# Recurrent gates of an encoder block: a full-height block-diagonal matmul against two 64-row halves

## The chip, the cores and the metric

The kernel runs on one core of one Trainium2 chip. The metric is the device time of one execution in microseconds (us), as the median of several executions. PE is the matrix engine (TensorE), PEld its weight loads, DVE the vector engine, ACT the scalar engine, POOL GpSimd, SP the engine that issues most DMAs. PSUM is the memory that PE writes its results to, eight banks of 128 partitions by 512 float32.

## What is computed

One layer of a streaming encoder on 512 frames of 1024 features: an RMS norm, one wide projection, a banded attention branch, a recurrent branch, a gated merge, and a SwiGLU feed-forward. The part that the change touches is the gates of the recurrent branch. The recurrent input (after a causal convolution of width 4) has 1024 features in 16 blocks of 64, and each gate multiplies each block by a 64 by 64 matrix of its own:

```
def rg_lru(x, w_r, b_r, w_i, b_i, lam):
    B, S, D = x.shape
    xb = x.reshape(B, S, N_RG_BLOCKS, RG_BLOCK)
    r = jax.nn.sigmoid(jnp.einsum('bsnd,nde->bsne', xb, w_r).reshape(B, S, D) + b_r)
    i = jax.nn.sigmoid(jnp.einsum('bsnd,nde->bsne', xb, w_i).reshape(B, S, D) + b_i)
    log_a = -RG_C * r.astype(jnp.float32) * jax.nn.softplus(-lam.astype(jnp.float32))
    a = jnp.exp(log_a)
    mult = jnp.sqrt(-jnp.expm1(2.0 * log_a))
    bx = mult * (i * x).astype(jnp.float32)
...
    _, h = lax.associative_scan(combine, (a, bx), axis=1)
    return h.astype(x.dtype)
```

## The kernel before

Features lie on partitions, frames along the free dimension. The 1024 features are eight feature tiles of 128 partitions, j = 0 to 7, so a feature tile holds two blocks of 64. Every product is made in three matmuls, because each float32 operand is kept as a rounded high part and a low remainder: high by high, high by low, low by high (`mm3`, L72 to L76). A projection of one feature tile is eight such triples, 24 matmuls of 128 rows by 512 columns into one PSUM bank.

**The recurrent stage.** The loop at L572 goes over j = 0, 2, 4, 6. For each it projects the recurrent input of two feature tiles (`xr`), convolves them (`rnn_conv`, L481: one ACT, three DVE instructions), and splits the result into a high part on ACT (L491) and a low part on POOL (L492), the tile `xch`. Then it projects the two GeLU gates (`gr`), and after each of them makes the recurrent gates of that feature tile (`rnn_gates`, L504). Then come the merge gates (`ga`, `gb`).

**The recurrent gates.** At setup the two gate weights are laid out as block-diagonal 128 by 128 matrices, one for each feature tile: a tile `wrg_raw` for each gate is set to zero on POOL (L322), two DMAs from SP fill the diagonal blocks (L324, L325), ACT rounds the whole tile to its high part (L470), and POOL subtracts to get the low part (L471). In `rnn_gates` each of the two gates takes one triple (L508) into a PSUM bank of its own (tag "s", two banks) and is read by one ACT instruction, a tanh with a bias from `hb` over 128 partitions by 512 (L510). After that ACT (L516, L517), DVE (L519 to L530) and POOL (L521, L535) make the recurrence out of it.

**PSUM.** One pool `ps` has four banks with the tag "mm", two with "t" (transposes and the `gr` projections), two with "s". The two "s" banks hold at first `gm_p` (the transposed norm gain, L379), then the gates, later the attention scores (L653), one of the feed-forward products (L275) and pieces of the output (L954).

**Order.** The instructions of an engine run in the order in which a planner has put them, from priorities and a model of the time; each then waits only for its own inputs and buffers. In the attention stage the order on PE is fixed by hand (L734). ACT, DVE and POOL work through their queues in order.

Also in `norm_half` (L343): the scaled input `xs` (DVE, L349) is transposed on PE (L357) into tiles with the tag "t", and split to `xnT` by ACT (L361) and DVE (L362).

Of the kernel before, what the change touches and what calls it, by code (L numbers as in the profile page):

```python
# [20 lines left out]
HD = 64  # L21
# [15 lines left out]
def block_kernel(ctx: ExitStack, tc: tile.TileContext, x, norm_mix_g, w_in, b_merge, rel_table,  # L37
# [3 lines left out]
    pe, dve, act, pool, sp = nc.tensor, nc.vector, nc.scalar, nc.gpsimd, nc.sync  # L41
# [9 lines left out]
    top = ctx.enter_context(pool_of("top", 1, "right"))  # L51
    top.tile([P, 120], F32, name="top_fill")
    cp = ctx.enter_context(pool_of("cp"))
    cp.tile([P, 48], F32, name="cp_fill")
    wp = ctx.enter_context(pool_of("wp", 2))
    tg_ = ctx.enter_context(pool_of("tg", 2))
    xn_stack, xnp = opened("xnT")
    nm_stack, nm = opened("norm")
# [1 line left out]
    qk_stack, qkp = opened("qk", 3, "right")  # L60
    z_stack, zp = opened("z", 1, "right")
    rw2_stack, rw2 = opened("rw2", 2, "right")
    ps = ctx.enter_context(tc.tile_pool(name="ps", bufs=2, space=PSUM))
    dr = ctx.enter_context(tc.tile_pool(name="dr", bufs=1, space=bass.MemoryType.DRAM))

    def f(ap):
        return ap.bitcast(F32)

    def mm_tile(name, tag="mm"):
        return ps.tile([P, S], F32, tag=tag, bufs=4 if tag == "mm" else 2, name=name)  # L70

    def mm3(o, sh, sl, mh, ml, start, stop, parts=False):  # L72

        pe.matmul(o, sh, mh, start=start, stop=False, skip_group_check=parts)  # L74
        pe.matmul(o, sh, ml, start=False, stop=False, skip_group_check=parts)  # L75
        pe.matmul(o, sl, mh, start=False, stop=stop, skip_group_check=parts)  # L76
# [194 lines left out]
    def block_product(name, i, right, c):  # L271

        w = weights(name)
        p = ps.tile([P, 256], F32, tag="mm", bufs=4, name=f"p_{name}")
        q = ps.tile([P, 2, 256], F32, tag="st"[i % 2], bufs=2, name=f"q_{name}")  # L275
# [40 lines left out]
    for t in range(2, NT):  # L316
        sp.dma_start(out=xt[t][:], in_=x[t * P:(t + 1) * P, :])
    load("gr0", 0)
    wrg_raw = []
    for name, w in (("r", w_rg_r), ("i", w_rg_i)):  # L320
        raw = nm.tile([P, 8, P], F32, name=f"wrg_raw_{name}")
        pool.memset(raw[:], 0.0)  # L322
        pairs = w.rearrange("(t two) d e -> two d t e", two=2)
        sp.dma_start(out=raw[0:64, :, 0:64], in_=pairs[0])  # L324
        sp.dma_start(out=raw[64:128, :, 64:128], in_=pairs[1])  # L325
        wrg_raw.append(raw)
    vr = nm.tile([NV, P], F32, name="vr")
    sp.dma_start(out=vr[V_CW:V_CW + 32, :], in_=conv_w.rearrange("w (t p) -> (w t) p", p=P))
    for at, vec, n in ((V_CB, conv_b, 8), (V_BR, b_rg_r, 8), (V_BI, b_rg_i, 8), (V_LAM, rg_lambda, 8), (V_BM, b_merge, 16),
# [46 lines left out]
        act.activation(junk[:], xt[t][:], AF.Square, accum_out=q[:])  # L376
        ssq.append(q[:])

    gm_p = ps.tile([P, S], F32, tag="s", bufs=2, name="gm_p")  # L379
    pe.transpose(gm_p[:, 0:8], gm_r[:], ident[0:8, 0:8])  # L380
    gm = cp.tile([P, 8], F32, name="gm")
    act.copy(gm[:], gm_p[:, 0:8])
    _, xnT = features(xnp, "xn", "xnT")
# [25 lines left out]
    pe.transpose(vp[:, 0:NV], vr[:], ident[0:NV, 0:NV])  # L409
    vc = cp.tile([P, NV], F32, name="vc")  # L410
    dve.tensor_copy(vc[:], vp[:, 0:NV])
    hb = cp.tile([P, 32], F32, name="hb")
    dve.tensor_scalar(hb[:, 0:16], vc[:, V_BR:V_BR + 16], 0.5, None, ALU.mult)
    dve.tensor_scalar(hb[:, 16:32], vc[:, V_BM:V_BM + 16], 0.5, None, ALU.mult)
    gf = vc[:, V_GF:V_GF + 8]


# [46 lines left out]
    sp2, spm4 = softplus_neg()  # L464


    wrg = []
    for name, raw in zip("ri", wrg_raw):
        hl = rw2.tile([P, 2, 8, P], F32R, bufs=1, name=f"wrg_{name}")
        act.activation(hl[:, 0], raw[:], AF.Copy)  # L470
        pool.tensor_sub(hl[:, 1], raw[:], f(hl[:, 0]))  # L471
        wrg.append(hl)

    nm_stack.close()

    rw_stack, rw = opened("rw", 2)


    u_pairs = []
# [22 lines left out]
        return g  # L502

    def rnn_gates(j, xc, xch, g):  # L504
        gates = []
        for n in range(2):
            po = ps.tile([P, S], F32, tag="s", bufs=2, name=f"rg{j}_{n}")
            mm3(po[:], wrg[n][:, 0, j], wrg[n][:, 1, j], xch[:, 0], xch[:, 1], True, True)  # L508
            gt = rw.tile([P, S], F32, tag=f"gt{n}", bufs=(2, 3)[n], name=f"gt{j}_{n}")
            act.activation(gt[:], po[:], AF.Tanh, bias=hb[:, 8 * n + j:8 * n + j + 1], scale=0.5)  # L510
            gates.append(gt)
        tr, ti = gates
        if j % 2 == 0:
            u_pairs.append(rw.tile([P, 2, S], F32, tag="u", bufs=2, name=f"u{j}"))
        u = u_pairs[-1][:, j % 2]
        act.activation(u, tr[:], AF.Tanh, bias=sp2[:, j:j + 1], scale=sp2[:, j:j + 1])  # L516
        act.activation(tr[:], tr[:], AF.Exp, bias=spm4[:, j:j + 1], scale=spm4[:, j:j + 1])  # L517

        dve.scalar_tensor_tensor(u, tr[:], 1.0, u, ALU.add, ALU.mult)  # L519
        a = rw.tile([P, S], F32, tag="a", bufs=3, name=f"a{j}")  # L520
        pool.tensor_scalar(a[:], u, -1.0, 1.0, ALU.mult, ALU.add)  # L521

# [49 lines left out]
    for j in range(0, KT, 2):  # L572
        for c in range(2):
            conv[j + c] = rnn_conv(j + c, tile_of(f"xr{j}", c, ahead=2))
        for c in range(2):
            po = tile_of(f"gr{j}", c, "mm" if j == 0 else "t")
# [13 lines left out]
    def halves(e):  # L590
        own, other = slice(e * HD, e * HD + HD), slice(HD - e * HD, 2 * HD - e * HD)
        return own, other


    qk = {}

# [48 lines left out]
    def scores(h):  # L645
        pr, e = divmod(h, 2)
        q, kh, kl = qk[pr]
        bias = bias_tile(h)
        lsum = cp.tile([P, NT], F32, tag="lsum", bufs=2, name=f"l{h}")
        nmax = cp.tile([P, NT], F32, tag="nmax", bufs=2, name=f"m{h}")  # L650
        rl = cp.tile([P, NT], F32, tag="rl", bufs=2, name=f"rl{h}")
        prob = [aw2.tile([P, (qb + 1) * P], F32, tag=f"p{qb}", name=f"p{h}_{qb}") for qb in range(NT)]
        banks = [ps.tile([P, S], F32, tag="s", bufs=2, name=f"s{h}_{i}") for i in range(2)] + [mm_tile(f"s{h}_2")]  # L653
        scs = [banks[0][:, 0:P], banks[0][:, P:3 * P], banks[1][:, 0:3 * P], banks[2][:]]
        for qb in range(NT):
            w = (qb + 1) * P
            qs = q[:, e, qb * P:(qb + 1) * P]
            pe.matmul(scs[qb], qs, kh[:, e, 0:w], start=True, stop=False)
            pe.matmul(scs[qb], qs, kl[:, e, 0:w], start=False, stop=True)
        for qb in range(NT):  # L660
            w = (qb + 1) * P
            dve.tensor_tensor_reduce(prob[qb][:], scs[qb], bias[:, S - w:S], -1.0, 3e38, ALU.add, ALU.min, nmax[:, qb:qb + 1])  # L662
            act.activation(prob[qb][:], prob[qb][:], AF.Exp, bias=nmax[:, qb:qb + 1], scale=-1.0, accum_out=lsum[:, qb:qb + 1])  # L663
        dve.reciprocal(rl[:], lsum[:])  # L664
        for qb in range(NT):
            pool.tensor_scalar(prob[qb][:], prob[qb][:], rl[:, qb:qb + 1], 1.0, ALU.mult, ALU.mult)  # L666
        return prob
# [283 lines left out]
    for cc, tags in enumerate(("mmmm", "sstmm")):  # L951

        pieces = [(t, every) for t in range(NT)] if cc == 0 else [*((t, every) for t in range(3)), (3, slice(0, CW)), (3, slice(CW, S))]
        pos = [ps.tile([P, S], F32, tag={"m": "mm"}.get(tag, tag), bufs=4 if tag == "m" else 2, name=f"po_out{cc}_{i}")  # L954
               for i, tag in enumerate(tags)]
        for k0 in ks[:late] if cc else ks:
            if cc == 0:
                for i in range(max(1, k0 // 2), min(k0 + 4, FT) // 2):
                    split_act(i)
            wf = weights(f"fo{cc}_{k0}", 3)  # L960
            for (t, at), po in zip(pieces, pos):
                out_tile(t, po, k0, wf, at)
        if cc == 0:
            for (t, at), po in zip(pieces, pos):
                h_out(0, t, po, pool, 0, at)
    wfs = [weights(f"fo1_{k0}", 0) for k0 in ks[late:]]
    for i, ((t, at), po) in enumerate(zip(pieces, pos)):
        for k0, wf in zip(ks[late:], wfs):
            out_tile(t, po, k0, wf, at)
        n = 1 + i // 4  # L970
# [30 lines left out]
```

## Time and profile before

| | us |
|---|---|
| median of 3 executions (881.80 to 882.15) | 881.89 |
| the profiled execution | 881.99 |
| its span, from the first instruction to the last | 880.2 |
| PE busy in the span | 869.7 |
| PE weight loads | 776.3 |
| DVE busy | 546.7 |
| ACT busy | 472.4 |
| POOL busy | 111.2 |
| DMA, mean over the span | 102 GB/s |

Busy time of PE is the union of its matmuls' records. A record is longer than the distance to the next one, since the matmuls are pipelined, so the distance between starts is the cost of one, and the length of the record is that plus a tail. The recurrent stage lies between about 34 and 180 us. The attention stage follows to about 440 us, the merge and the feed-forward take the rest.

### The profile page before, as it was taken

The numbers are of one execution on the slowest core, as the hardware profiler recorded it, in microseconds if no ns is written. First come the engines' busy times: TensorE is split into PE (matmuls) and PEld (weight loads), VectorE is DVE, ScalarE is ACT, GpSimd is POOL, SyncE is SP. The second block draws the span as 40 slices with busy tenths as digits, with TensorE's granted clock in tenths as the row PEclk, the third lists the DMA queues.
The fourth block names the chain that finished last, engine by engine and source line by source line (L and its number), as shares of the span: only waits on it lengthen the run. The fifth ranks groups of instructions, "written<-read, shape, count | busy, mean of one in ns | idle before, by whom it ended". The sixth has DMA issues, their size and how long they took to land.

```text
span 880.2 us, 13310 instructions
## 1 busy us (share of the span) xinstructions
PE 869.7 (99%) x5220; PEld 776.3 (88%) x5220; DVE 546.7 (62%) x856; ACT 472.4 (54%) x823; POOL 111.2 (13%) x141
## 2 busy tenths in 40 slices
PE   8999999999999999999999999999999999999997
PEld 5988888888888999988888889999999999888886
DVE  5776557663366676665556557888888887554203
ACT  7666656662256776666533366555555555723103
POOL 4013211220011222322100000000000001301100
PEclk9999999999999999999999999999999999999999
DMA  8223232433342232321223630433333332353002
GB/s 268 82 87 98 93 96 81 136 96 95 101 139 74 89 90 83 86 73 60 73 96 114 245 95 27 144 95 121 98 96 99 117 121 73 127 182 121 25 1 96
DMA packets 86079, 90.10 MB, mean 102 GB/s; under 512 B 5376, under 2 KB 74608, under 8 KB 86016
## 3 DMA queue, kind: packets, MB, share of 16 engines
q1 hardware_dynamic: 84640, 85.78, 31.4%
q10 hardware_dynamic: 1376, 3.47, 1.0%
q8 instruction: 41, 0.67, 0.3%
q14 instruction: 22, 0.18, 0.1%
HBM read 87.10 MB, written 2.14 MB: 101 GB/s over the span
## 4 chain that ended last, share of the span: by engine, by line
PE 97%; DVE 1%; ACT 1%; issue 1%; DMA 0%; ACTq 0%
PE po_out L74 5%; PE po_out L76 5%; PE po_out L75 5%; PE p_fg L74 2%; PE o L697 2%; PE p_fg L76 2%; PE p_fu L76 2%; PE p_fu L75 2%; PE p_fg L75 2%; PE p_fu L74 2%; PE pT L677 2%; PE po_v L74 2%; PE po_v L76 2%; PE po_v L75 2%; PE po_ga L74 2%; PE po_q L74 2%
## 5 line engine op out<-in xcount | busy, mean ns | idle before, releaser
L75 PE MATMUL po_out<-whl_fo,act_hi 128*128 128x512 f32 (+1 forms) x198 | 72.5, 366 | 0.0
L74 PE MATMUL po_out<-whl_fo,act_hi 128*128 128x512 f32 (+1 forms) x198 | 72.3, 366 | 0.0
L76 PE MATMUL po_out<-whl_fo,act_lo 128*128 128x512 f32 (+1 forms) x198 | 71.7, 365 | 0.0
L666 POOL TENSOR_SCALAR p<-p,rl 128x128 f32<-128x128 f32 (+1 forms) x64 | 39.7, 638 | 128.8 <-DVE rl L664 128.5
L81 DVE TENSOR_TENSOR whl_fo<-raw_fo,whl_fo 128x1024 fp32r<-128x1024 f32 x22 | 27.8, 1274 | 44.2 <-ACT whl_fo L80 43.8
L885 POOL TENSOR_TENSOR act_lo<-act,act_hi 128x1024 fp32r<-128x1024 f32 x4 | 10.9, 2716 | 323.5 <-ACT act_hi L884 321.5
L80 ACT ACTIVATE whl_fo<-raw_fo 128x1024 fp32r<-128x1024 f32 x22 | 23.0, 1058 | 49.0 <-PE po_out L76 34.6
L663 ACT ACTIVATE p<-p,m 128x128 f32<-128x128 f32 (+1 forms) x64 | 35.8, 560 | 16.1 <-DVE m L662 16.1
L76 PEld LDWEIGHTS po_out<-whl_fo,act_lo 128*128 128x128 f32 x198 | 37.3, 189 | 6.0
L75 PEld LDWEIGHTS po_out<-whl_fo,act_hi 128*128 128x128 f32 x198 | 37.4, 189 | 5.9
L74 PEld LDWEIGHTS po_out<-whl_fo,act_hi 128*128 128x128 f32 x198 | 37.4, 189 | 5.9
L74 PE MATMUL po_v<-whl_v,xnT 128*128 128x256 f32 x128 | 36.8, 287 | 0.0
L76 PE MATMUL po_v<-whl_v,xnT 128*128 128x256 f32 x128 | 36.2, 283 | 0.0
L75 PE MATMUL po_v<-whl_v,xnT 128*128 128x256 f32 x128 | 36.2, 283 | 0.0
L81 DVE TENSOR_TENSOR pp<-pT,pp 128x384 fp32r<-128x384 f32 (+1 forms) x48 | 27.9, 598 | 8.5 <-ACT pp L80 8.5
L662 DVE CUSTOM_DVE_ANT_0 p<-s,bias 128x128 f32<-128x128 f32 (+1 forms) x64 | 29.1, 484 | 0.0
L75 PE MATMUL po_xr<-xnT,whl_xr 128*128 128x512 f32 (+1 forms) x80 | 27.9, 354 | 0.6 <-DVE xnT L362 0.6
L81 DVE TENSOR_TENSOR whl_fg_s<-s_fg,whl_fg_s 128x1024 fp32r<-128x1024 f32 x20 | 25.6, 1294 | 3.7 <-ACT whl_fg_s L80 3.7
L74 PE MATMUL po_gr<-xnT,whl_gr 128*128 128x512 f32 (+1 forms) x80 | 27.8, 349 | 0.1
L76 PE MATMUL po_gr<-xnT,whl_gr 128*128 128x512 f32 (+1 forms) x80 | 27.5, 348 | 0.3 <-DVE whl_gr L81 0.3
L75 PE MATMUL po_gr<-xnT,whl_gr 128*128 128x512 f32 (+1 forms) x80 | 27.6, 347 | 0.0
L81 DVE TENSOR_TENSOR whl_qk<-raw_qk,whl_qk 128x1024 fp32r<-128x1024 f32 x16 | 20.8, 1298 | 10.8 <-ACT whl_qk L80 10.8
(352 smaller groups left out, 3041.1 us busy)
## 6 DMA issues: line engine op xcount, KB each, us to landing
raw_fg<-in_w_ffn_in_dram SPq DMA_DIRECT2D x24, 512.0 KB, 4.1
raw_fu<-in_w_ffn_in_dram SPq DMA_DIRECT2D x22, 512.0 KB, 3.7
raw_fo<-in_w_ffn_out_dram SPq DMA_DIRECT2D x22, 512.0 KB, 4.1
raw_qk<-in_w_in_dram SPq DMA_DIRECT2D x32, 256.0 KB, 3.7
raw_xr<-in_w_in_dram SPq DMA_DIRECT2D x8, 512.0 KB, 4.6
raw_gr<-in_w_in_dram SPq DMA_DIRECT2D x8, 512.0 KB, 3.4
raw_ga<-in_w_in_dram SPq DMA_DIRECT2D x8, 512.0 KB, 3.9
raw_gb<-in_w_in_dram SPq DMA_DIRECT2D x8, 512.0 KB, 3.4
```

The lines of the kernel that those rows point to most:

```text
L74: pe.matmul(o, sh, mh, start=start, stop=False, skip_group_check=parts)
L75: pe.matmul(o, sh, ml, start=False, stop=False, skip_group_check=parts)
L76: pe.matmul(o, sl, mh, start=False, stop=stop, skip_group_check=parts)
L80: act.activation(hi, src, AF.Copy)
L81: dve.tensor_sub(lo, src, f(hi))
L662: dve.tensor_tensor_reduce(prob[qb][:], scs[qb], bias[:, S - w:S], -1.0, 3e38, ALU.add, ALU.min, nmax[:, qb:qb + 1])
L663: act.activation(prob[qb][:], prob[qb][:], AF.Exp, bias=nmax[:, qb:qb + 1], scale=-1.0, accum_out=lsum[:, qb:qb + 1])
L666: pool.tensor_scalar(prob[qb][:], prob[qb][:], rl[:, qb:qb + 1], 1.0, ALU.mult, ALU.mult)
L677: pe.transpose(pt[:, at * P:(at + 1) * P], prob[qb][:, kb * P:(kb + 1) * P], ident[:])
L697: pe.matmul(po[:, S - n:S], st, pp[i][:, part, lo:lo + n], start=kb == 0 and part == 0, stop=kb == NT - 1 and part == 1)
L885: (pool if i in (0, 1, 2, 4) else dve).tensor_sub(lo[:], o[:], f(hi[:]))
```

## The change

The two blocks of a feature tile are no longer one block-diagonal matrix of 128 rows. Block e (0 or 1) lies on rows 64e to 64e+63. Its weights for both gates stand side by side on these rows, 64 columns for each gate, so that one matmul of 64 rows and 128 columns gives both gates of one block. For block 0 the gate r has the columns 0 to 63, for block 1 the columns 64 to 127, so r of a block always comes out on the partitions where the block's features lie, and i on the other 64.

For each feature tile there are six matmuls again: the three products of the splitting, each for the two blocks, alternating between the rows 64 to 127 and the rows 0 to 63. The results go to a tile of two PSUM banks, one bank for each block, out of a pool of its own (`rg`, one buffer). The order of the six on PE is fixed, and the products with the low part of `xch` come first. The two gates are read by four ACT instructions of 64 partitions where there were two of 128; those for i read from one half of the partitions and write to the other, with a copy of the bias that is swapped in the same way (eight more columns of `hb`, two more small DVE copies).

One weight tile of 128 by 8 by 128 takes the place of two. The two POOL memsets go, the four DMAs stay, and one ACT rounding and one POOL subtraction remain of two each. The PSUM banks of the gates are given back after the recurrent stage to a pool `ss`, which the attention scores and the later users of "s" use. `gm_p` moves to a "t" bank. Two small constant tiles (`cp_fill`, `hb`) change their widths so that the memory behind them keeps its place.

```diff
-    cp.tile([P, 48], F32, name="cp_fill")
+    cp.tile([P, 40], F32, name="cp_fill")
...
-    ps = ctx.enter_context(tc.tile_pool(name="ps", bufs=2, space=PSUM))
+    ps = ctx.enter_context(tc.tile_pool(name="ps", bufs=2, space=PSUM, reuse_waits="tile"))
+    rg_stack = ExitStack()
+    rgp = rg_stack.enter_context(tc.tile_pool(name="rg", bufs=1, space=PSUM, reuse_waits="tile"))
...
-    wrg_raw = []
-    for name, w in (("r", w_rg_r), ("i", w_rg_i)):
-        raw = nm.tile([P, 8, P], F32, name=f"wrg_raw_{name}")
-        pool.memset(raw[:], 0.0)
+    wrg_raw = nm.tile([P, 8, P], F32, name="wrg_raw")
+    for n, w in enumerate((w_rg_r, w_rg_i)):
         pairs = w.rearrange("(t two) d e -> two d t e", two=2)
-        sp.dma_start(out=raw[0:64, :, 0:64], in_=pairs[0])
-        sp.dma_start(out=raw[64:128, :, 64:128], in_=pairs[1])
-        wrg_raw.append(raw)
+        for e in range(2):
+            at = slice(HD * (n ^ e), HD * (n ^ e) + HD)
+            sp.dma_start(out=wrg_raw[e * HD:e * HD + HD, :, at], in_=pairs[e])
...
-    gm_p = ps.tile([P, S], F32, tag="s", bufs=2, name="gm_p")
+    gm_p = ps.tile([P, S], F32, tag="t", bufs=2, name="gm_p")
...
-    hb = cp.tile([P, 32], F32, name="hb")
+    hb = cp.tile([P, 40], F32, name="hb")
...
+    for to, of in ((slice(0, HD), slice(HD, P)), (slice(HD, P), slice(0, HD))):
+        dve.tensor_copy(hb[to, 32:40], hb[of, 8:16])
...
-    wrg = []
-    for name, raw in zip("ri", wrg_raw):
-        hl = rw2.tile([P, 2, 8, P], F32R, bufs=1, name=f"wrg_{name}")
-        act.activation(hl[:, 0], raw[:], AF.Copy)
-        pool.tensor_sub(hl[:, 1], raw[:], f(hl[:, 0]))
-        wrg.append(hl)
+    wrg = rw2.tile([P, 2, 8, P], F32R, bufs=1, name="wrg")
+    act.activation(wrg[:, 0], wrg_raw[:], AF.Copy)
+    pool.tensor_sub(wrg[:, 1], wrg_raw[:], f(wrg[:, 0]))
...
-        gates = []
-        for n in range(2):
-            po = ps.tile([P, S], F32, tag="s", bufs=2, name=f"rg{j}_{n}")
-            mm3(po[:], wrg[n][:, 0, j], wrg[n][:, 1, j], xch[:, 0], xch[:, 1], True, True)
-            gt = rw.tile([P, S], F32, tag=f"gt{n}", bufs=(2, 3)[n], name=f"gt{j}_{n}")
-            act.activation(gt[:], po[:], AF.Tanh, bias=hb[:, 8 * n + j:8 * n + j + 1], scale=0.5)
-            gates.append(gt)
-        tr, ti = gates
+        pos = rgp.tile([P, 2, S], F32, tag="rg", bufs=1, name=f"rg{j}")
+        with tc.manual_schedule(engines={mybir.EngineType.PE}):
+            for i, (w, x_) in enumerate(((0, 1), (0, 0), (1, 0))):
+                for e in (1, 0):
+                    rows = slice(e * HD, e * HD + HD)
+                    pe.matmul(pos[:, e], wrg[rows, w, j], xch[rows, x_], start=i == 0, stop=i == 2)
+        tr, ti = (rw.tile([P, S], F32, tag=f"gt{n}", bufs=(2, 3)[n], name=f"gt{j}_{n}") for n in range(2))
+        for e in range(2):
+            own, other = halves(e)
+            act.activation(tr[own, :], pos[own, e], AF.Tanh, bias=hb[own, j:j + 1], scale=0.5)
+            act.activation(ti[own, :], pos[other, e], AF.Tanh, bias=hb[other, 32 + j:33 + j], scale=0.5)
...
+    rg_stack.close()
+    ss = ctx.enter_context(tc.tile_pool(name="ss", bufs=2, space=PSUM, reuse_waits="tile"))
```

More of the change, by code (lines that the diff above doesn't have):

```diff
@@ L274, in block_product @@
         p = ps.tile([P, 256], F32, tag="mm", bufs=4, name=f"p_{name}")
-        q = ps.tile([P, 2, 256], F32, tag="st"[i % 2], bufs=2, name=f"q_{name}")
+        q = (ss, ps)[i % 2].tile([P, 2, 256], F32, tag="st"[i % 2], bufs=2, name=f"q_{name}")
         a, b = (tg_.tile([P, 2, 256], F32, tag="tg", name=f"keep{n}_{name}") for n in "ab")
@@ L464, in block_kernel, with halves @@
     sp2, spm4 = softplus_neg()
-    wrg = []
-    for name, raw in zip("ri", wrg_raw):
-        hl = rw2.tile([P, 2, 8, P], F32R, bufs=1, name=f"wrg_{name}")
-        act.activation(hl[:, 0], raw[:], AF.Copy)
-        pool.tensor_sub(hl[:, 1], raw[:], f(hl[:, 0]))
-        wrg.append(hl)
+    wrg = rw2.tile([P, 2, 8, P], F32R, bufs=1, name="wrg")
+    act.activation(wrg[:, 0], wrg_raw[:], AF.Copy)
+    pool.tensor_sub(wrg[:, 1], wrg_raw[:], f(wrg[:, 0]))
     nm_stack.close()
     rw_stack, rw = opened("rw", 2)
+    def halves(e):
+        own, other = slice(e * HD, e * HD + HD), slice(HD - e * HD, 2 * HD - e * HD)
+        return own, other
     u_pairs = []
@@ L588, in backwards @@
         return blocks(ap)[:, :, ::-1]
-    def halves(e):
-        own, other = slice(e * HD, e * HD + HD), slice(HD - e * HD, 2 * HD - e * HD)
-        return own, other
     qk = {}
@@ L652, in scores @@
         prob = [aw2.tile([P, (qb + 1) * P], F32, tag=f"p{qb}", name=f"p{h}_{qb}") for qb in range(NT)]
-        banks = [ps.tile([P, S], F32, tag="s", bufs=2, name=f"s{h}_{i}") for i in range(2)] + [mm_tile(f"s{h}_2")]
+        banks = [ss.tile([P, S], F32, tag="s", bufs=2, name=f"s{h}_{i}") for i in range(2)] + [mm_tile(f"s{h}_2")]
         scs = [banks[0][:, 0:P], banks[0][:, P:3 * P], banks[1][:, 0:3 * P], banks[2][:]]
@@ L953, in block_kernel @@
         pieces = [(t, every) for t in range(NT)] if cc == 0 else [*((t, every) for t in range(3)), (3, slice(0, CW)), (3, slice(CW, S))]
-        pos = [ps.tile([P, S], F32, tag={"m": "mm"}.get(tag, tag), bufs=4 if tag == "m" else 2, name=f"po_out{cc}_{i}")
+        pos = [(ss if tag == "s" else ps).tile([P, S], F32, tag={"m": "mm"}.get(tag, tag), bufs=4 if tag == "m" else 2, name=f"po_out{cc}_{i}")
                for i, tag in enumerate(tags)]
```

## The prediction

> **What bounds the kernel now.** I read the page from the top: the span, the busy shares, the granted clock, then the chain that ended last.
>
> ```profile
> span 880.2 us, 13310 instructions
> PE 869.7 (99%) x5220; PEld 776.3 (88%) x5220; DVE 546.7 (62%) x856; ACT 472.4 (54%) x823; POOL 111.2 (13%) x141
> PEclk9999999999999999999999999999999999999999
> PE 97%; DVE 1%; ACT 1%; issue 1%; DMA 0%; ACTq 0%
> ```
>
> The reader is to see that PE is busy in 99% of the span, at full clock, and makes 97% of the chain. A busy PE can still hide slack, so next come the stage that changes (the busy times by stretch, whose columns are the length, then PE, PEld, DVE, ACT and POOL with their counts, the clock, DMA) and the waits of PE.
>
> ```profile
> 44.00:66.00 22.00, 22.00 (x99) 18.23 (x98) 16.37 (x33) 13.80 (x18) 2.54 (x3) 1.00 0.27 87
> 66.00:88.00 22.00, 22.00 (x99) 18.23 (x98) 14.50 (x18) 14.40 (x20) 7.55 (x5) 1.00 0.34 98
> 132.00:154.00 22.00, 22.00 (x99) 18.23 (x98) 15.97 (x19) 14.02 (x18) 3.91 (x3) 1.00 0.26 80
> 176.00:880.00 704.00, 697.71 (x4375) 633.55 (x4373) 434.07 (x693) 362.86 (x667) 72.28 (x104) 1.00 0.32 99
> ...
> PE busy L305 <- DVE eps_t L311: 1.2, 1, 1.2
> PE po_xr L74 <- ACT xnT L361: 0.8, 2, 0.4
> PE pt_mix L357 <- DVE xs_mix L349: 0.6, 1, 0.6
> PE po_xr L75 <- DVE xnT L362: 0.6, 1, 0.6
> ```
>
> In the recurrent stage PE never stops, 99 matmuls in each 22 us, so 0.22 us for one. No other engine is above 16.4 of 22 us. The four longest waits of PE make 3.2 us, all of them at the start; the others are 0.5 us or less. So time taken off PE in this stage should come off the end, as long as its inputs follow.
>
> **The gates as they are.** PE in order of time around the gates of feature tile 2 (start, length, line, operation):
>
> ```profile
> 79.80 0.39 PE L74 MATMUL rg<-xch,wrg_r 128*128 128x512 f32 x1
> 80.03 0.39 PE L75 MATMUL rg<-xch,wrg_r 128*128 128x512 f32 x1
> ...
> 80.94 0.39 PE L76 MATMUL rg<-xch,wrg_i 128*128 128x512 f32 x1
> 81.16 0.39 PE L74 MATMUL po_gr<-xnT,whl_gr 128*128 128x512 f32 x1
> ...
> 300.29 0.28 PE L74 MATMUL po_v<-whl_v,xnT 128*128 128x256 f32 x1
> 300.41 0.28 PE L75 MATMUL po_v<-whl_v,xnT 128*128 128x256 f32 x1
> ...
> 27.03 0.47 PEld L357 LDWEIGHTS pt_mix<-ident,xs_mix 128*128 128x128 f32 x4
> ```
>
> The six gate matmuls of a feature tile take 81.16 - 79.80 = 1.36 us, 0.226 us each; the other 0.16 us of a record (0.39 - 0.226) is a tail that the next matmul covers. Eight feature tiles cost 8 x 1.36 = 10.9 us of PE, all on the path. With 256 columns the distance is 0.12 us, and the last row has four weight loads in 0.47 us: each is 0.14 long (0.19 in the other stages), so their distance is (0.47 - 0.14) / 3 = 0.11 us. A new weight load, of 128 columns as here, can thus go in every 0.11 to 0.12 us.
>
> **The change on PE.** Still six matmuls of 512 columns and six weight loads of 128 columns for each feature tile. But two neighbours use different rows of the array, different rows of `xch` and different banks, and no sum joins them. The trace shows no two matmuls that stream side by side, so the bounds are: no overlap, 6 x 0.226 = 1.36 us as now; full overlap, 3 x 0.226 = 0.68 us plus little. With overlap the weight loads come next: one each 0.11 us starts the six matmuls 0.11 us apart, and the group lasts 5 x 0.11 + 0.226 = 0.78 us. I take 0.78, a saving of 0.58 us for each feature tile, 4.6 us for eight. (The Trainium skill, "TensorE: Matmul & The Clock Gate", Part 3, has matmuls on different row groups run concurrently, and gives 3.07 times for four of 32 rows; no row here shows it.)
>
> **The switch.** Each group is entered from a full-height matmul and left to one: 16 switches, if the groups stay whole. The only short-row matmul of the trace is the transpose of the norm gain, eight rows high:
>
> ```profile
> 7.17 0.22 PE L380 MATMUL gm_p<-ident,gm_r 8*128 8x8 f32 x1
> 7.32 0.66 PE L357 MATMUL pt_mix<-ident,xs_mix 128*128 128x128 f32 x4
> ```
>
> The full-height transpose behind it starts 0.15 us later; between ordinary transposes it is 0.11, so this switch shows 0.04 us at least. The upper end is a full emptying: the tail of 0.16 us, plus 0.11 us if the next weights can't be loaded ahead, 0.27. I take 0.10 us, between this row and the tail alone. 16 x 0.10 = 1.6 us. Bounds: 0.6 to 4.3 us. The Trainium skill speaks against the change here: "TensorEngine Tiling (Array Packing)", Key Properties, says that a change of tiling mode drains the TensorE. By that rule the switch costs 0.16 to 0.27 us; the gm_p row, whose successor starts before its modelled end (7.17 + 0.22 = 7.39), doesn't agree, though it is one row of an idle moment.
>
> Net on PE: 4.6 - 1.6 = **3.0 us**.
>
> **ACT, and the buffers.** Rows of the readers, and of a 64-partition instruction of the same length from the attention stage:
>
> ```profile
> L510 ACT ACTIVATE gt<-rg,hb x16: 671/690/692, 46.4 to 170.4; 128x512 f32<-128x512 f32 x16
> L698 ACT ACTIVATE oacc<-o x16: 590/594/598, 262.7 to 437.9; 64x512 f32<-64x512 f32 x16
> L491 ACT ACTIVATE xch<-xc x8: 612/632/632, 38.9 to 160.8; 128x512 fp32r<-128x512 f32 x8
> ...
> L74 PE MATMUL po_yb<-rnn,whl_yb x64: 389/389/397, 197.1 to 247.0; 128*128 128x512 f32 x64
> ```
>
> Half the partitions cost the same (594 ns against 632), so 32 tanh replace 16, 16 x 0.69 = 11.0 us more of ACT, 1.4 us for each feature tile. ACT has 22 - 14.4 = 7.6 us of each 22 us free at its fullest, and gets 1.4 to 2.8 us more there. So it is hidden, and I cost it at nothing. Bare, it would cost up to 11 us. Queued behind these tanh on ACT are the L516 and L517 instructions, and the weight splits that feed PE. The gates' results are wanted late: the last tanh starts at 170.4 us, the projection that reads the branch (`po_yb`) at 197. One buffer of two banks means that a group waits for all four tanh of the group before it (2.8 us); the groups are a projection, 24 x 0.226 = 5.4 us, or more apart. Hidden too. The products with the low part come first, so a group starts only when POOL has made it, and shouldn't then be broken up.
>
> **The start.** POOL loses two memsets and one subtraction, ACT one rounding:
>
> ```profile
> L322 POOL MEMSET wrg_raw_i<- x1: 951/951/951, 1.8 to 1.8; 128x1024 f32 x1
> L470 ACT ACTIVATE wrg_i<-wrg_raw_i x1: 1079/1079/1079, 16.9 to 16.9; 128x1024 fp32r<-128x1024 f32 x1
> 19.12 2.84 POOL L471 TENSOR_TENSOR wrg_i<-wrg_raw_i,wrg_i 128x1024 fp32r<-128x1024 f32 x1
> 6.38 0.75 DVE L349 TENSOR_SCALAR xs_mix<-x,rs_mix 128x1024 f32<-128x1024 f32 x1
> 17.04 2.68 DVE L349 TENSOR_SCALAR xs_mix<-x,rs_mix 128x1024 f32<-128x1024 f32 x1
> 17.12 1.30 DVE xs_mix L349
> 8.37 0.14 ACT L382 COPY gm<-gm_p 128x8 f32<-128x8 f32 x1
> 32.88 0.17 DVE L413 TENSOR_SCALAR hb<-vc 128x16 f32<-128x16 f32 x1
> ```
>
> The same DVE scaling takes 0.75 us alone and 2.68 us beside POOL's subtractions, and PE then waits 0.6 us for `xnT`, which stands behind it. One subtraction less can take back none to all of that wait, and up to the 1.3 us of the chain's piece of it; I take 0.3 us. Against it: `gm_p` takes one of the two "t" banks until ACT has copied it at 8.37 + 0.14 us, so two of the first four transposes (7.32 us) move behind it, 2 x 0.11 = 0.2 us. The memsets (0.95 us each, the second from 1.8 us) and the two DVE copies (about 0.17 us each, at 33 us beside a busy PE) gate nothing. The four DMAs are the same in SP's queue. Sum: 0.1 us gained, bounds -0.5 and +1.3.
>
> **Sum.** 3.0 + 0.1 = 3.1 us from the profiled execution's 881.99 us, which is 0.1 above the median: 878.9 there, **878.8** as a median.
>
> **Rivals.** *The switch takes it back*: at 0.27 us, 16 cost 4.3, so 0.3 + 0.1 us remain: 881.5. For it: the tail is real work in the array; against it: the gm_p row. At 0.16 us (2.6) it would be 879.8, still faster. *The halves don't overlap* (the slower side): the six keep their 1.36 us, and 16 switches at 0.10 to 0.27 come on top, 1.6 to 4.3 us, the middle 884.8. It decides from the point where the six take more than 1.36 - 2 x 0.10 = 1.16 us, 0.19 us each. For it: nothing in the trace shows overlap; against: separate rows, banks and sums. *ACT arrives late*: around the first two feature tiles weight splits and tanh follow one another on ACT,
>
> ```profile
> 52.64 1.05 ACT L80 ACTIVATE whl_xr<-raw_xr 128x1024 fp32r<-128x1024 f32 x1
> 53.59 1.25 ACT L510 ACTIVATE gt<-rg,hb 128x512 f32<-128x512 f32 x2
> ...
> 63.48 0.39 PE L74 MATMUL po_xr<-xnT,whl_xr 128*128 128x512 f32 x1
> ```
>
> and a split pushed back by two tanh could hold PE for 1.4 us a time, twice, 2.8 us: 881.6. Against: the `xr` matmuls that want this split start at 63.5 us, 10 us behind it. *It doesn't do what it says*: the matmuls go through the whole array as before, no gain, no switch: 881.8.
>
> **How the numbers follow.** Forecast 0.64 (876.0 to 880.1 by its bounds: group 0.70, switch 0.04 and start +1.3 give 0.66 x 8 - 0.6 + 1.3 = 6.0 us); switch 0.17; no overlap 0.09; ACT 0.05; nothing 0.05. A measurement of this kernel tells about 0.2%, 1.8 us, from no change, so faster is below 880.1: the forecast and a little of the second, 0.66; slower above 883.7: most of the no-overlap case, 0.08; the rest, 0.26, between. The range leaves out the no-overlap case and the tails: 876.0 to 882.0.
>
> **What would show it.** Right: gate matmuls starting about 0.11 us apart on PE, 0.7 to 0.8 us from the first of a group to its last start plus 0.226, gaps of about 0.1 us at its edges, and the rest of PE unmoved. Wrong: starts 0.226 us apart (no overlap); 0.2 us or more lost at each edge (the drain); other matmuls between the six, which adds switches; or new waits of PE on ACT between 44 and 180 us. The DVE scaling at 17 us should shrink if the POOL argument holds.

## The result and the profile after

The changed kernel takes **878.96 us** (median of six executions, 878.91 to 879.11) against 882.13 us for the kernel before on the same chip (six executions, 881.80 to 883.05). The ratio is 0.9963, its 95% interval 0.9950 to 0.9976: some 3.2 us faster. The forecast was 878.8 us, in a range of 876.0 to 882.0. The profiled execution took 878.95 us, 3.04 us less than that of before. The sum came out, but two of its terms were each about a microsecond off, in opposite directions, and one of these came about by another path than the forecast had. Most of what follows is about them.

The page of the kernel after, from the top: span, busy shares, and the engines' shares of the chain that ended last.

```profile
span 877.2 us, 13330 instructions
PE 868.0 (99%) x5220; PEld 770.6 (88%) x5220; DVE 544.0 (62%) x858; ACT 483.6 (55%) x838; POOL 105.8 (12%) x138
PE 97%; ACT 1%; DVE 1%; DMA 0%; issue 0%; ACTq 0%
```

The span is 3.0 us shorter (880.2 before). The bound is unchanged: as many matmuls, PE busy 99%, 97% of the chain. ACT gained 11.2 us of work, and that is nowhere in the time.

**Where the time went.** PE in order of time: the first matmul of the merge gates `ga`, ahead of the first recurrent gates, and the first of the query projection behind the last. First the kernel before, then the kernel after; columns are start, length, engine, line, operation, and in brackets the idle time ahead of it with what ended it.

```profile
38.91 0.47 PE L74 MATMUL po_ga<-xnT,whl_ga 128*128 128x512 f32 x1 [0.33 <-DVE sp_p L451]
...
180.44 0.39 PE L74 MATMUL po_q<-xnT,whl_qk 128*128 128x512 f32 x1
```

```profile
37.76 0.47 PE L76 MATMUL po_ga<-xnT,whl_ga 128*128 128x512 f32 x1 [0.33 <-DVE sp_p L453]
...
177.49 0.39 PE L76 MATMUL po_q<-xnT,whl_qk 128*128 128x512 f32 x1
```

These two marks hold all eight groups of gates and nothing else that changed on PE: the other 576 matmuls between them are the same, in the same order. The stretch between them took 141.53 us before and 139.73 after: **1.80 us come from the gates**. The first mark is reached at 37.76 instead of 38.91: **1.15 us come from the start**. Together 2.95 of the 3.04 us; behind the second mark hardly anything changes.

**A group of six.** PE of the kernel after around the gates of feature tile 2, then the same window cut so that only the first two, and only the first four, of the six are in it:

```profile
77.98 0.39 PE L78 MATMUL po_gr<-xnT,whl_gr 128*128 128x512 f32 x1
78.30 0.96 PE L514 MATMUL rg<-xch,wrg 64*128 64x512 f32 x6
79.19 0.50 PE L76 MATMUL po_gr<-xnT,whl_gr 128*128 128x512 f32 x1
...
81.83 0.39 PE L78 MATMUL po_gr<-xnT,whl_gr 128*128 128x512 f32 x1
```

```profile
78.30 0.50 PE L514 MATMUL rg<-xch,wrg 64*128 64x512 f32 x2
```

```profile
78.30 0.73 PE L514 MATMUL rg<-xch,wrg 64*128 64x512 f32 x4
```

The two halves do stream side by side. Two records together last 0.50 us, and the longest single gate record is 0.497 (next fence), so both start within 0.01 us of each other. Four last 0.73 and six 0.96: each further pair adds 0.23 us, the distance of one full-height matmul. Six matmuls take three slots.

The edges cost more than the inside. The last full-height matmul starts at 77.98, and its slot of 0.226 us ends at 78.21, but the first gates start at 78.30: 0.09 us of gap. Then their records are 0.50 long instead of 0.39: the 0.11 us of a weight load is inside, because it did not go ahead of time. The same on the way out: the group's third slot ends at 78.30 + 0.11 + 3 x 0.23 = 79.10, the next full-height record starts at 79.19, 0.09 later, and is again 0.50 long. So each edge costs about 0.20 us.

From the start of the last full-height matmul to that of the next, less the weight load inside its record, it is 79.19 + 0.11 - 77.98 = 1.32 us. Before it was seven slots, 7 x 0.226 = 1.58. That is 0.26 us for each feature tile and 2.1 for eight. The missing 0.3 us lie behind the groups: from 79.30 to 81.83 eleven matmuls start 0.230 us apart instead of 0.226, 0.04 us for each group. The eight groups agree in these distances to some 0.002 us.

**ACT.** The gate tile's groups, with the first and last start, in the kernel after:

```profile
L514 PE MATMUL rg<-xch,wrg x48: 386/394/497, 43.4 to 167.7; 64*128 64x512 f32 x48
L518 ACT ACTIVATE gt<-rg,hb x16: 665/684/685, 45.2 to 169.6; 64x512 f32<-64x512 f32 x16
L519 ACT ACTIVATE gt<-rg,hb x16: 682/682/687, 45.9 to 170.3; 64x512 f32<-64x512 f32 x16
```

Half the partitions cost the same 0.68 us, twice as often. Busy times by stretch over the recurrent stage (length; then PE, PEld, DVE, ACT, POOL with their counts), before and after:

```profile
44.00:176.00 132.00, 132.00 (x584) 109.35 (x583) 83.93 (x113) 80.65 (x106) 26.75 (x23) 1.00 0.32 99
```

```profile
44.00:176.00 132.00, 132.00 (x592) 105.35 (x589) 80.70 (x109) 93.33 (x122) 25.10 (x23) 1.00 0.31 96
```

ACT goes from 80.65 to 93.33 us of 132, and PE is never idle in either. The 12.7 us more lie wholly beside PE.

**The start.** DVE of the kernel before: the splits of the two halves of `whl_gr`, and what stands right ahead of the scaling of `xs_mix` (17.04 us, 2.68 long). Then DVE and POOL of the kernel after:

```profile
15.45 1.21 DVE L81 TENSOR_TENSOR whl_gr<-raw_gr,whl_gr 128x1024 fp32r<-128x1024 f32 x1
...
16.66 0.46 DVE L362 SCALAR_TENSOR_TENSOR xnT<-pt_mix,gm,xnT 128x256 fp32r<-128x256 f32 x1
...
20.43 2.62 DVE L81 TENSOR_TENSOR whl_gr<-raw_gr,whl_gr 128x1024 fp32r<-128x1024 f32 x1
```

```profile
16.57 0.85 DVE L362 SCALAR_TENSOR_TENSOR xnT<-pt_mix,gm,xnT 128x256 fp32r<-128x256 f32 x2
17.35 2.78 DVE L349 TENSOR_SCALAR xs_mix<-x,rs_mix 128x1024 f32<-128x1024 f32 x1
...
20.45 1.21 DVE L83 TENSOR_TENSOR whl_gr<-raw_gr,whl_gr 128x1024 fp32r<-128x1024 f32 x1
```

```profile
17.18 2.40 POOL L471 TENSOR_TENSOR wrg<-wrg_raw,wrg 128x1024 fp32r<-128x1024 f32 x1 [2.67 <-ACT wrg L470]
```

Before, POOL's second subtraction ran from 19.12 to 21.96 us, right behind the first, and two DVE instructions fell beside the two: the scaling of `xs_mix` (2.68 us) and the later split of `whl_gr` (2.62, where the earlier one took 1.21). After, one subtraction remains, from 17.18 to 19.58. It still covers the scaling, which stays at 2.78 us; the split behind it is free and takes 1.21, so DVE gains 1.41 us there.

The matmuls of the kernel before did not wait for that later split, though. Two waits of PE in the kernel before, and the first matmul of the projection that reads the later split, before and after:

```profile
16.72 0.39 PE L76 MATMUL po_gr<-xnT,whl_gr 128*128 128x256 f32 x1 [0.26 <-DVE whl_gr L81]
...
20.17 0.39 PE L75 MATMUL po_xr<-xnT,whl_xr 128*128 128x256 f32 x1 [0.56 <-DVE xnT L362]
...
22.98 0.36 PE L74 MATMUL po_gr<-xnT,whl_gr 128*128 128x256 f32 x1
```

```profile
21.84 0.36 PE L76 MATMUL po_gr<-xnT,whl_gr 128*128 128x256 f32 x1
```

Before, PE comes to this projection at 22.98 us, when the split is all but done (20.43 + 2.62 = 23.05); the first matmul that needs it starts at 23.54, without a wait. After, PE is there at 21.84, 1.14 us sooner, which is the whole 1.15 of the first mark. So the time was lost ahead of it, and most of it in the two waits: 0.26 us for the earlier split and 0.56 for the `xnT` that stands behind the slow scaling. The kernel after hardly waits at either place (0.03 us and nothing). Its scaling is as slow, but two pieces of `xnT` go ahead of it on DVE where one did. Why the planner put them so was not followed.

### The profile page after: what moved, and what is told of

The parts are those of the page before. It is cut to its first block, busy times and chain, and to the rows that moved or that the text cites. A ratio compares the mean times of both kernels' runs of the same rounds, so it can differ in the third digit from the quotient of the medians.

```text
span 877.2 us, 13330 instructions
## 1 busy us (share of the span) xinstructions
PE 868.0 (99%) x5220; PEld 770.6 (88%) x5220; DVE 544.0 (62%) x858; ACT 483.6 (55%) x838; POOL 105.8 (12%) x138
## 4 chain that ended last, share of the span: by engine, by line
PE 97%; ACT 1%; DVE 1%; DMA 0%; issue 0%; ACTq 0%
PE po_out L76 5%; PE po_out L77 5%; PE po_out L78 5%; PE p_fg L76 2%; PE o L702 2%; PE p_fg L78 2%; PE p_fu L78 2%; PE p_fg L77 2%; PE p_fu L77 2%; PE p_fu L76 2%; PE pT L682 2%; PE po_v L76 2%; PE po_v L78 2%; PE po_v L77 2%; PE po_gb L77 2%; PE po_ga L76 2%
```

## The experiments

Two questions: does the group really cost three slots plus two edges of 0.20 us, and does the second POOL subtraction, put back, take the 1.15 us of the start away again? The rival for the first was that neighbouring matmuls overlap by their order; for the second, that the memsets, the second rounding or chance moved the start. Edits are against the kernel after unless said otherwise; ratios are to the kernel before, with 95% intervals; "the stretch" is the one between the two marks.

**Half by half.** The three matmuls of rows 64 to 127 are issued first, then the three of rows 0 to 63, so only the middle two are neighbours on different rows.

```diff
-            for i, (w, x_) in enumerate(((0, 1), (0, 0), (1, 0))):
-                for e in (1, 0):
+            for e in (1, 0):
+                for i, (w, x_) in enumerate(((0, 1), (0, 0), (1, 0))):
```

> The same six gate matmuls, ordered as three on the rows 64 to 127 and then three on the rows 0 to 63. If neighbours on different rows stream side by side, only the third and the fourth can now do so, a group takes five slots where it took three, and eight groups cost 2 x 0.233 x 8 = 3.7 us more than the changed kernel: 882.7 us, about the time of the kernel before. If the gain has nothing to do with neighbours on different rows, the time stays at 879.0.

Measured 879.13 us, ratio 0.9963 (0.9950 to 0.9975): no change against the kernel after. PE around the same group:

```profile
78.18 0.39 PE L78 MATMUL po_gr<-xnT,whl_gr 128*128 128x512 f32 x1
78.50 0.97 PE L514 MATMUL rg<-xch,wrg 64*128 64x512 f32 x6
79.40 0.50 PE L76 MATMUL po_gr<-xnT,whl_gr 128*128 128x512 f32 x1
```

Six in 0.97 us, as three pairs, although the order given was three and three. My expectation missed: the overlap doesn't need neighbours in the order of issue. Each half works through its own matmuls, and the alternation in the changed kernel is worth nothing by itself.

**All six on one half.** Block 1's matmuls use the rows of block 0 too, so the odd blocks' gates are computed from the even blocks. Same count, same two banks, same switches, but no second half.

```diff
-                    rows = slice(e * HD, e * HD + HD)
+                    rows = slice(0, HD)
```

> All six gate matmuls of a feature tile on the rows 0 to 63, so the gates of the odd blocks are computed from the even blocks' data and weights. The number of matmuls and of switches stays. If two matmuls on different halves stream side by side and two on the same half don't, a group takes six slots instead of three: 3 x 0.233 x 8 = 5.6 us more, 884.6 us, with starts 0.233 us apart. If the gain came from anything else than side-by-side streaming (smaller weight loads, the order, the setup), 879.0.

Measured 884.47 us, ratio 1.0027 (1.0018 to 1.0036). The same group of this run:

```profile
79.30 0.39 PE L78 MATMUL po_gr<-xnT,whl_gr 128*128 128x512 f32 x1
79.61 1.66 PE L514 MATMUL rg<-xch,wrg 64*128 64x512 f32 x6
81.20 0.50 PE L76 MATMUL po_gr<-xnT,whl_gr 128*128 128x512 f32 x1
```

Six slots, 1.66 us instead of 0.96, and 5.5 us more in all. This is the no-overlap rival of the prediction, made real: slower than before. It shows that the rows of the two halves carry the gain, not the banks or the shape.

**Two feature tiles in one group.** If a switch costs 0.20 us, half of them should go when two feature tiles share a group. The second tile's results go to two "mm" banks. First for all four pairs of tiles:

```diff
+        gate_pos.update(gate_matmuls(j))
+        for c in range(2):
...
-            for i, (w, x_) in enumerate(((0, 1), (0, 0), (1, 0))):
+            for j in (j0, j0 + 1):
+                xch = conv[j][1]
+                for i, (w, x_) in enumerate(((0, 1), (0, 0), (1, 0))):
```

> The gate matmuls of two feature tiles in one group of twelve, the second tile's results in two banks of the tag mm: eight switches between full-height and half-height matmuls where there were sixteen. At the 0.20 us that the edges of a group show in the trace after, 8 x 0.20 = 1.6 us less: 877.3 us. At the 0.10 us of the prediction 0.8 less: 878.2. If the edges are no price of the switch, 879.0, and more if the two borrowed banks make PE wait.

Measured 887.82 us, ratio 1.0061 (1.0048 to 1.0073): slower. The waits of PE in this run (who waited, for whom; us in total, times, longest):

```profile
PE rg L518 <- DVE sp_p L452: 5.4, 1, 5.4
PE rg L518 <- POOL xch L496: 2.3, 1, 2.3
```

The first pair needs the convolution of both tiles, which hangs on the setup at the start, so PE stood for 7.7 us. And behind the waits PE ran at half speed: from 42 to 52 us the granted clock is 0.50, and the first matmuls of `po_ga` start 0.43 us apart instead of 0.226, until 53.3 us. The edit had a cost that I had not counted. So the pairing was kept for the later tiles only, where the inputs are there:

```diff
+            if j == 0:
+                gate_pos.update(gate_matmuls(c))
+                gates_of(c)
+        if j:
+            gate_pos.update(gate_matmuls(j, j + 1))
+            for c in range(2):
+                gates_of(j + c)
```

> As the run with two feature tiles in one group, but the first two feature tiles keep groups of their own, since there PE waited for their inputs. Six switches fewer than the changed kernel. From the stretch of the earlier run that had no waits (three pairs 1.37 us shorter), 0.23 us a switch: 878.96 - 1.37 = 877.6 us. At the prediction's 0.10 us, 878.4. If merging itself makes PE wait, above 879.0.

Measured **877.62 us**, ratio 0.9946 (0.9933 to 0.9958), the fastest version of the study. PE at the first mark, around a group of two tiles, and at the second mark:

```profile
37.69 0.47 PE L76 MATMUL po_ga<-xnT,whl_ga 128*128 128x512 f32 x1 [0.33 <-DVE sp_p L453]
...
83.34 0.39 PE L78 MATMUL po_gr<-xnT,whl_gr 128*128 128x512 f32 x1
83.66 1.65 PE L522 MATMUL rg<-xch,wrg 64*128 64x512 f32 x12
85.24 0.50 PE L76 MATMUL po_ga<-xnT,whl_ga 128*128 128x512 f32 x1
...
176.03 0.39 PE L76 MATMUL po_q<-xnT,whl_qk 128*128 128x512 f32 x1
```

Twelve matmuls in one group, six slots in 1.65 us, with the same edges. The stretch takes 138.34 us, 1.39 less than in the kernel after. Three pairs save six switches: 0.23 us each, close to the 0.20 of an edge and half of the 0.04 behind a group.

**High parts first.** Does the low part's place in the group matter? With it last, a group could start before POOL is done and be broken up.

```diff
-            for i, (w, x_) in enumerate(((0, 1), (0, 0), (1, 0))):
+            for i, (w, x_) in enumerate(((0, 0), (1, 0), (0, 1))):
```

> The changed kernel with the products of the high part of the convolved input first and that of the low part (made by POOL) last. In the built order the first group is split in two by two other matmuls, the others stay whole: two more switches, 2 x 0.20 = 0.4 us, so 879.4 us; if PE also waits for POOL inside groups, up to 1.3 us more for each group that does.

Measured 879.44 us, ratio 0.9966 (0.9954 to 0.9978), not to be told from the kernel after by the time alone. The first group of its profiled run:

```profile
43.77 0.73 PE L514 MATMUL rg<-xch,wrg 64*128 64x512 f32 x4
44.44 0.50 PE L76 MATMUL po_ga<-xnT,whl_ga 128*128 128x512 f32 x1
44.77 0.40 PE L77 MATMUL po_ga<-xnT,whl_ga 128*128 128x512 f32 x1
45.10 0.50 PE L514 MATMUL rg<-xch,wrg 64*128 64x512 f32 x2
```

Two projections got between four and two of the gates, and the stretch is 140.10 us, 0.37 more: two switches at 0.19. The other seven groups stay whole, so the order is worth a few tenths, by its first group. (The profiled execution was the longest of the six, 880.41 us; its first mark comes 1.06 us later than in the kernel after, ahead of all the gates.)

**The setup done twice.** For the start: a second rounding and a second subtraction, into a tile that nothing reads.

```diff
+    again = rw2.tile([P, 2, 8, P], F32R, bufs=1, name="again")
+    act.activation(again[:, 0], wrg_raw[:], AF.Copy)
+    pool.tensor_sub(again[:, 1], wrg_raw[:], f(again[:, 0]))
```

> The changed kernel with a second ACT rounding and a second POOL subtraction of the gate weights into a tile that nobody reads, so that the setup has as much ACT and POOL work as before. If the lighter setup gave the 1.15 us by which the merge gates start earlier (37.76 us against 38.91), 880.1 us, with the DVE instructions around 17 to 23 us as slow as before. If the whole gain is the gate matmuls', 879.0.

Measured 880.22 us, ratio 0.9973 (0.9963 to 0.9983): 1.26 us of the gain gone. `po_ga` starts at 38.80, close to the 38.91 of before, and the stretch stays at 139.71. Memsets and `gm_p` are as in the kernel after, so they are not what was lost here. Which of the two instructions is it? One at a time:

```diff
+    again = rw2.tile([P, 2, 8, P], F32R, bufs=1, name="again")
+    pool.tensor_sub(again[:, 1], wrg_raw[:], f(wrg[:, 0]))
```

> The changed kernel with a second POOL subtraction at the start, into a tile that nobody reads, but no second ACT rounding. If the POOL subtraction beside DVE is what the lighter setup saved, about 880.2 us, as with both, and the DVE split of the second half of the gr weights at 20 us takes about 3 us instead of 1.2. If the ACT rounding was it, 879.0.

```diff
+    again = rw2.tile([P, 2, 8, P], F32R, bufs=1, name="again")
+    act.activation(again[:, 0], wrg_raw[:], AF.Copy)
```

> The changed kernel with a second ACT rounding at the start, but no second POOL subtraction. If the POOL subtraction is the cause, 879.0 us; if ACT's 1.05 us is, 880.2. If the planner takes another order at the start, either can be missed by some us, as in two runs so far.

The subtraction alone: 880.43 us, ratio 0.9977 (0.9968 to 0.9986). The rounding alone: 879.37, ratio 0.9968 (0.9955 to 0.9980). POOL, DVE and PE of the run with the second subtraction, then DVE of the run with the second rounding:

```profile
19.40 2.86 POOL L473 TENSOR_TENSOR again<-wrg_raw,wrg 128x1024 fp32r<-128x1024 f32 x1
```

```profile
20.32 3.02 DVE L83 TENSOR_TENSOR whl_gr<-raw_gr,whl_gr 128x1024 fp32r<-128x1024 f32 x1
```

```profile
23.40 0.39 PE L78 MATMUL po_gr<-xnT,whl_gr 128*128 128x256 f32 x1 [0.97 <-DVE whl_gr L83]
```

```profile
20.68 1.21 DVE L83 TENSOR_TENSOR whl_gr<-raw_gr,whl_gr 128x1024 fp32r<-128x1024 f32 x1
```

With POOL busy from 19.40 to 22.26, the split of `whl_gr` takes 3.02 us instead of 1.21, and PE then waits 0.97 us for just this split. With the rounding alone it takes 1.21. The two medians, from one chip, differ by 1.06 us. That is the chain in this order of the start: POOL subtraction, DVE split, PE. It shows that one more subtraction is enough to take the gain away again. It does not show that the kernel before lost its time in this way: there PE came too late to wait for the split, and lost about as much at the two waits ahead of it.

**The last subtraction off POOL.** If one subtraction less is worth 1.15 us, the remaining one, which still holds the scaling at 2.78 us, might be worth more. DVE takes it, where the same length of split costs 1.21:

```diff
-    pool.tensor_sub(wrg[:, 1], wrg_raw[:], f(wrg[:, 0]))
+    dve.tensor_sub(wrg[:, 1], wrg_raw[:], f(wrg[:, 0]))
```

> The changed kernel with the subtraction of the gate weights at the start on DVE instead of POOL. If DVE is slow at 17 us because POOL's subtraction runs beside it, the DVE scaling of 2.78 us becomes 0.75, and the subtraction takes about 1.2 us of DVE; PE no longer stands behind either, so 878.0 to 879.0. If the scaling is slow for another reason, it stays at 2.78 and the time rises by up to 1.2 us.

Measured 881.42 us, ratio 0.9995 (0.9986 to 1.0003): the expectation missed. DVE, then the longest wait of PE in this run:

```profile
17.61 0.74 DVE L349 TENSOR_SCALAR xs_mix<-x,rs_mix 128x1024 f32<-128x1024 f32 x1
```

```profile
PE po_ga L76 <- ACT whl_gb L82: 2.3, 1, 2.3
```

The scaling falls from 2.78 to 0.74 us, as said. But the planner, given other instructions, put ACT's work at the start in another order, and PE now waits 2.3 us for a weight split: `po_ga` starts at 40.00. The stretch is 139.75, unchanged. What one part gains at the start, another order loses. The profiled execution kept a clock of 1.00 through this wait. Over the eleven executions the time goes with the clock granted in the span: 880.85 to 881.42 us at 0.998 or 0.999, 882.42 to 882.76 at 0.996 or 0.997. Together with the later pairing of tiles it was no better:

> Both of the last two edits. If they are independent, the sum of their differences to the changed kernel: about 877 us. If the order of the work at the start changes for the worse, as in the run with half the setup, above 879.0.

Measured 881.23 us (eleven executions, 879.44 to 882.18), ratio 0.9984 (0.9975 to 0.9993). The stretch of the profiled run is 138.35 us, so the pairing is worth its 1.4 us here too; `po_ga` starts there at 39.78 instead of 37.76, and the start takes it back. At a granted clock of 0.999 this version took 879.44 to 879.65 us, which is about the sum of the two differences (877.62 + 881.0 - 878.96 = 879.7, with the 881.0 of the other run at its higher clock); the other seven executions, at 0.995 to 0.997, took 881.04 to 882.18. The expectation of 877 missed, because the second edit was a loss by itself.

**The kernel before with less setup.** The other way round: the memset, DMAs, rounding and subtraction of gate i are left out of the kernel before, and gate i is made from the weights of gate r.

```diff
-    for name, w in (("r", w_rg_r), ("i", w_rg_i)):
+    for name, w in (("r", w_rg_r),):
...
-            mm3(po[:], wrg[n][:, 0, j], wrg[n][:, 1, j], xch[:, 0], xch[:, 1], True, True)
+            mm3(po[:], wrg[0][:, 0, j], wrg[0][:, 1, j], xch[:, 0], xch[:, 1], True, True)
```

> The kernel before with its full-height gate matmuls, but with the weights of gate r used for both gates: gate i's memset, two DMAs, rounding and subtraction are left out, so gate i is computed from the wrong weights. PE has the same work. If the lighter setup is worth 1.15 us by itself, 881.0 us; if its gain in the changed kernel was an accident of the order of the work, 882.1.

Measured 885.72 us, ratio 1.0033 (1.0021 to 1.0046): slower, with less to do.

```profile
PE po_ga L74 <- ACT whl_gb L80: 2.8, 1, 2.8
```

The same wait as above, from another order at the start, and the first mark comes 2.74 us later than in the kernel before (41.65). But the stretch behind it, with the same matmuls, takes 143.17 us instead of 141.53. One of its first matmuls, and the busy times of two microseconds there (length; PE, PEld, DVE, ACT and POOL with their counts, then the granted clock and DMA):

```profile
42.62 0.63 PE L76 MATMUL po_ga<-xnT,whl_ga 128*128 128x512 f32 x1
```

```profile
42.00:44.00 2.00, 2.00 (x6) 1.54 (x6) 2.00 (x4) 0.84 (x2) 1.70 (x1) 0.50 0.59 206
```

Behind the wait the granted clock is 0.50, a record lasts 0.63 us instead of 0.39, and the first eight matmuls start 0.43 us apart instead of 0.226, until 45.1 us. That is the other 1.64 us. So a wait of PE cost more than its length here, and in the run with all pairs; in the profiled execution of the run with the subtraction on DVE, a wait of 2.3 us did not.

This run says nothing on the worth of the setup. It does say that the order which the planner finds at the start, with the clock behind it, moves this kernel by about as much as the change does. Why it chose so was not followed, and a start ordered by hand was not tried.

## Why the prediction came out, point by point

**PE is the bound, and time taken off it comes off the end**: right. The marks moved by 2.95 us and the execution by 3.04.

**Overlap of the two halves**: right, and shown by the run with all six on one half. The size was a little off the other way: 0.69 us for six (3 x 0.23) instead of 0.78. The stagger of 0.11 us for each weight load, taken from a row of loads into the whole array, isn't there. PEld of the kernel after has six loads in one group of 0.53 us,

```profile
78.30 0.53 PEld L514 LDWEIGHTS rg<-xch,wrg 64*128 64x128 f32 x6 [0.35 <-issue]
```

where loads of 0.19 us started one by one, 0.11 apart, would need 5 x 0.11 + 0.19 = 0.74. The halves load side by side, too.

**The switch at 0.10 us**: this is the term that failed, and the sign that the prediction named for it, 0.2 us or more lost at each edge, came. It measured 0.20 at each edge, and 0.23 by the experiment with six fewer. Of the upper end of the bounds, the 0.11 us for a weight load that can't go ahead is there in full, and of the tail of 0.16 some 0.09. The mistake was to lean to the `gm_p` row: eight columns wide, in an idle moment, with little in flight that had to end first, it could not show what a switch costs between full-size matmuls. Among bounds from a row that is alike in name and a sum that is alike in mechanism, the sum was the better guide. The Trainium skill, "TensorEngine Tiling (Array Packing)", Key Properties, has the array drain at a change of mode. These rows fit it in part: nothing goes ahead over an edge, and it costs 0.20 us; but the gates start at 78.30, before the record of the last full-height matmul ends (77.98 + 0.39 = 78.37, a modelled end), so they do not show that the array is empty.

**Net 3.0 us on PE**: 1.80. The group gave 0.09 us more for each tile than taken, the switches 0.20 less (two edges), and the matmuls behind a group 0.04 less: -0.15 for each, -1.2 us for the eight.

**ACT hidden**: right; 12.7 us more in the stage, no wait of PE on it.

**Groups stay whole with the low part first**: right; the opposite order broke up the first.

**The start at +0.1 us**: +1.15, within bounds of -0.5 to +1.3, but not by the step that was argued. The prediction had one subtraction less shorten the scaling of `xs_mix`, and so the 0.6 us wait for the `xnT` behind it; it took 0.3 us of that. The scaling stayed at 2.78 us, because the remaining subtraction is the one beside it. The wait went all the same, because in the new order that piece of `xnT` stands ahead of the scaling, and the 0.26 us for the earlier split went too. The subtraction that is gone freed the next instruction on DVE, the later split of `whl_gr`. Its 2.62 us, against 1.21 five microseconds earlier, stood in the trace of before, and I hadn't looked beside the *second* subtraction. It is worth 1.06 us in the order of the kernel after, where PE is early enough to wait for it; in the kernel before it cost PE nothing. Whether the order of before, with one subtraction less, would have gained as much was not shown: the one run that tried it got a third order. The Trainium skill, "SBUF — State Buffer", section "Who interferes with whom", has a DVE instruction with two inputs in SBUF contend with a GpSimd instruction that reads SBUF. The trace agrees: the split takes 1.21 us alone, 2.62 to 3.02 beside POOL.

**`gm_p` in a "t" bank at 0.2 us**: nothing was lost. The first projection on PE, in the kernel before and in the kernel after:

```profile
9.62 0.50 PE L74 MATMUL po_xr<-xnT,whl_xr 128*128 128x256 f32 x2 [0.41 <-ACT xnT L361]
```

```profile
9.54 0.50 PE L76 MATMUL po_xr<-xnT,whl_xr 128*128 128x256 f32 x2 [0.19 <-ACT xnT L361]
```

It starts at 9.54 us instead of 9.62, and waits for ACT's split in either case. Two of the first four transposes did move behind the copy (7.66 us, then 8.47), at no cost that shows.

**The rivals**: the switch came three quarters of the way to its rival price, 0.20 of 0.27, and without the start the time would have been about 880.1, at the edge of the 1.8 us that the prediction took a measurement to tell. No overlap, a late ACT, and no effect didn't happen.

So the total of 3.1 us was met partly by luck: -1.2 on PE and +1.05 at the start, the second by an order of the instructions that had not been forecast.

## What to carry to other kernels

A matrix with two diagonal blocks is worth splitting over two row halves when the group between two switches is long: here each edge of a group costs nearly one matmul of 512 columns, so six matmuls save three slots and lose almost two at the edges, while twelve in one group save six for the same two. Put as many short-row matmuls together as their inputs allow, but not where PE would then stand and wait for the last of them. When work goes from POOL, look at what DVE does beside each of the instructions that go, and then whether PE is early enough to wait for it: the same split, slow beside POOL, cost PE nothing in the kernel before and 0.97 us in the run with a second subtraction.

## What the hardware showed that was not expected

- The two halves of the array run their matmuls independently. Issued as three and three, they took the time of three pairs (six in 0.97 us), as in the alternating order.
- A switch between full-height and 64-row matmuls costs 0.20 us on either side, and for the eleven matmuls behind a group the distance is 0.230 us instead of 0.226. What this last part comes from stayed open.
- Behind some waits of PE at the start the granted clock fell to 0.50 for some microseconds, and 512 columns took 0.43 us instead of 0.226: 1.6 us behind a wait of 2.8 us. Behind a wait of 2.3 us in another trace it did not fall. What decides it stayed open.
- A DVE instruction that runs into a POOL subtraction looks held until POOL is done, not slowed in part. The scaling takes 0.74 us without and 2.78 beside one: POOL ends at 17.18 + 2.40 = 19.58, 0.74 more is 20.32, and the scaling ends at 20.13. The split of the run with a second subtraction: 19.40 + 2.86 = 22.26, 1.21 more is 23.47, and it ends at 23.34.
